# A second tile for turned exponentials, their split one step later, and a fourth tile for first weight parts in the first mixer

## The chip, the cores and the metric

The kernel runs on one core of one Trainium2 chip. The metric is the device time of one execution, in microseconds; the times shown are medians of several executions. A core has five engines with a list of instructions each: TensorE (PE in the profile, its weight loads PEld), VectorE (DVE), ScalarE (ACT), GpSimd (POOL) and SyncE (SP). An engine works through its list in order, and waits on semaphores for what other engines or transfers deliver.

## The reference

Two layers of a decoder trunk for 256 tokens of width 2048, in float32. Each layer adds a mixer and then a gated feed-forward network to the residual stream:

```
for l in range(2):
    h = rms_norm(x, mix_norm[l])
    h = mixer_ab(h, ...) if l == 0 else mixer_c(h, ...)
    x = x + h
    h = rms_norm(x, ffn_norm[l])
    x = x + conv_ffn(h, ...)
```

`mixer_ab` projects to 6144 columns. One half of it is a gated unit that mixes tokens within chunks of 128 (8 heads), the other a gated linear recurrence (8 heads of 128). `mixer_c` is softmax attention with 16 heads of 128, normalised queries and keys, a forgetting gate that adds differences of a cumulative sum `c` to the scores, and an output gate:

```
s = q @ k.T * scale + c[query] - c[key]
p = softmax(where(causal, s, -inf))
o = (p @ v) * sigmoid(g)
```

## The kernel before, in words

**Weights and accuracy.** TensorE multiplies in a rounded float32 format. To keep accuracy, each factor is split into a rounded first part and a remainder, and three of the four products are added. Weights come in chunks of 128 x 1024 numbers (512 KB): SP issues the load into a tile `w` (L191), ScalarE rounds it into `wh` (L178), VectorE subtracts to get the remainder `wl` (L179), and TensorE then runs twelve matmuls of 512 columns on the chunk (L305 to L307 or L324 to L326), four of each kind. The tiles of a chunk are handed out by `three` (L164): four `w`, three `wh` and three `wl` in turn. In mixer C and in the feed-forward layers `deep` names a further pool, and some chunks take tiles from it: in mixer C every fourth chunk takes its `wh` and `wl` there (`more` is 1).

**The clock of the kernel.** Side work is written as Python generators. `tick` (L128) is called once ahead of each chunk and advances each generator in flight by one step, at most `depth[0]` of them at once. So a `yield` is one chunk of weights, and `LAG` (6) of them are left between the issue of a move and the first use of what it brings.

**The order of the lists.** A planner draws up each engine's list at compile time from the order in the program, which acts as priority, and from estimated times. Three helpers add order edges: `in_order` keeps the weight parts in sequence, `held` (L368) puts an instruction behind the last `wh` or `wl` that the program has issued so far, and `tied` puts small matmuls behind the last large one. On the chip the lists are fixed and only semaphores decide.

**First mixer.** `project_first` computes the first projection while the input still arrives. Then follow `mixes` (squares for a norm in a tile `junk`, L557), eight recurrences `hgrn` with products on VectorE and small copies `E` on ScalarE (L695), whose matmuls are L712, L719 and L741 to L743, and `values` (L762), whose projection reads activations in reversed order from a tile `ar` that GpSimd copies. This mixer has no further pool for weight tiles.

**Mixer C.** Four groups of four heads. A group projects queries, keys and values, eight chunks each. Query and key pieces are copied from PSUM to `z` (L1079), squared into `junk` and summed (`sumsq`, L396), scaled, transposed in blocks of 32 by VectorE into `tmp` (L337) and moved into `turn` by sixteen small transfers that SP and GpSimd share (L344). `sums` (L914) makes the cumulative sum `fc` of the forgetting gate once, in small rows; for these it takes two tiles of the tag `pt`. `columns` (L953) turns `fc` with TensorE.

`attend` (L964) handles two heads, in this order of steps: split queries and keys; scores on TensorE, then maximum, exponentials and sums into `sc` (L996 to L1007); two steps on, VectorE transposes blocks of `sc` into `ptmp` (L1014); a step later GpSimd issues sixteen moves from `ptmp` to `pt` (L1023), which make up the turned exponentials; `LAG - 1` steps on, ScalarE and VectorE split them into `ph` and `pl` (L1032, L1033); a step later TensorE multiplies them with the values (L1041, L1044) and ScalarE copies out `o` (L1047). Pairs begin `PAIR` (5) ticks apart. There is one `ptmp`, one `ph`, one `pl` and two `pt`.

Then come four pieces of the output gate (`gate` waits until all heads are done), the output projection and the second feed-forward layer.

Of the kernel before, what the change touches and what calls it, by code (L numbers as in the profile page):

```python
# [8 lines left out]
F32 = mybir.dt.float32  # L9
F32R = mybir.dt.float32r  # L10
# [44 lines left out]
def tile_trunk(ctx: ExitStack, tc: tile.TileContext, x, pp_d, cst_d, mlev_d, msk_d,  # L55
# [107 lines left out]

    def three(n):  # L164
        deep["turn"] += 1
        wpool, pool, nw, ns = wp, wp, 4, 3
        if deep["pool"] is not None:
            if deep["more"] == 2 and deep["turn"] > 12 and deep["turn"] % 5 in (1, 3):
                wpool, pool, nw, ns = deep["pool"], deep["pool"], 2, 2
            elif deep["more"] == 1 and deep["turn"] % 4 == 3:  # L170
                pool, ns = deep["pool"], 1
        w = wpool.tile([P, n], F32, tag="w", name=nm("w"), bufs=nw)
        wh = pool.tile([P, n], F32R, tag="wh", name=nm("wh"), bufs=ns)
        wl = pool.tile([P, n], F32R, tag="wl", name=nm("wl"), bufs=ns)
        return w, wh, wl

# [298 lines left out]
    def mixer_ab(norm):  # L475
# [21 lines left out]
        for g, ps in enumerate(project_first(w_v, norm, lambda: queue.append(finish()))):  # L497
# [5 lines left out]
            else:  # L503
                drain()
                Rt = norm.Rt
                last = ps
        A = norm.a

        def fetch_late(*args):
            r = SC.dma_start(*args)  # L510
# [38 lines left out]
        def mixes():  # L549
            for g in (1, 0):  # L550
                yield
                for T in range(2):
                    held(act(gv[g][:, T], last[T] if g else gv[0][:, T], AF.Gelu, scale=Rt[:, T:T + 1]))
            for g in (1, 0):
                for T in range(2):
                    i = (2 * g + T) * 4
                    j = hp.tile([P, 512], F32, tag="junk", name=nm("junk"), bufs=1)  # L557
                    held(V.tensor_tensor(j, gv[g][:, T], gv[g][:, T], ALU.mult), "wl")
                    V.tensor_reduce(ss[:, i:i + 4], j.rearrange("p (h d) -> p h d", d=P), AX.X, ALU.add)
                    yield  # L560
            yield
            rsq(ss[:, 0:2 * NH], ss[:, 0:2 * NH], P)
            bound()
            for g in range(2):
                yield
                for T in range(2):
                    i = (2 * g + T) * 4
                    v4 = gv[g][:, T].rearrange("p (h d) -> p h d", d=P)
                    held(V.tensor_tensor(v4, v4, ss[:, i:i + 4].unsqueeze(2).to_broadcast([P, 4, P]),
                                         ALU.mult), "wl")  # L570
            yield
            yield
            for h in range(0, NH, 2):
                ps = bank()
                both = [mix(h + i, ps[:, i * S:(i + 1) * S]) for i in range(2)]
                for m in both:
                    next(m)
                for m in both:
                    next(m, None)
                yield  # L580
# [179 lines left out]
        gz = []  # L760

        def values(j):  # L762
            ps = project_tok(w_i[j], norm, lambda: hp.tile([P, 512], F32R, tag="ar", name=nm("ar"), bufs=2))
            itok = hp.tile([P, 2, 512], F32, tag="tok", name=nm("itok"), bufs=2)
            for T in range(2):
                SC.activation(itok[:, T], ps[T], AF.Copy, scale=Rr[:, T:T + 1])
            itoks.append((itok, steps[0]))
# [82 lines left out]
        for q in range(4):  # L850
            if q == 0:

                ps = stretch(0, (0, 2, 4, 6, 8, 10), more=True)
                ahead = stretch(1, (0, 2, 4, 6), more=True)
                stretch(0, (12, 14), ps=ps)
            elif q == 1:
                ps = stretch(1, (8, 10, 12, 14), ps=ahead)
            else:
                ps = stretch(q, range(0, KT, 2))
            z = hp.tile([P, 2, 512], F32, tag="tok", name=nm("zo"), bufs=2)  # L860
            tmp = hp.tile([P, 1024], F32, tag="E", name=nm("tmp"), bufs=2)
            dst = wide("dst").rearrange("p (m t) -> p m t", m=4)
            if q == 0:
                depth[0] = 2
            add_four(q, ps, z, tmp, dst, nxt, 2 if q in (1, 2) else 1, (nc.sync, nc.gpsimd) if q else (nc.gpsimd,))
        es.close()
        banks(ctx, 4)
        return nxt
# [2 lines left out]
    def mixer_c(norm):  # L871
# [39 lines left out]
                PE.matmul(ps[r:r + CH, 0:S], w2[:, k], xT[k], start=k < 4, stop=k >= KT - 4, skip_group_check=True)  # L911
            return ps, pr

        def sums(ps, pr, fc):  # L914
            yield
            yield
            Rq = hp.tile([P, LANE], F32, tag="Rq", name="Rq")
            rows = [hp.tile([P, 6, P], F32, tag="pt", name=nm("rows"), bufs=2)[0:CH].rearrange("p m q -> p (m q)")
                    for _ in range(2)]
            f, fa, on = (rows[0][:, i * S:(i + 1) * S] for i in range(3))  # L920
            R = rows[1][:, 2 * S:3 * S]
            c = rows[1][:, 0:2 * S].rearrange("p (g n) -> p g n", g=2)
            rsq(Rq, pr[:, 0:LANE], D)
            for g in range(4):
                SC.activation(R[:, LANE * g:LANE * (g + 1)], Rq[BLK * g:BLK * g + CH], AF.Copy)
            for g, t in ((1, c[:, 0]), (2, c[:, 1]), (3, f)):
                r = SC.activation(t, ps[BLK * g:BLK * g + CH, 0:S], AF.Copy)
                if g == 1:
                    held(r)
            yield  # L930
            held(V.tensor_tensor(f, ps[0:CH, 0:S], f, ALU.add), "wl")
            for g in range(2):
                V.tensor_tensor(f, f, c[:, g], ALU.add)
            V.memset(fc, 0.0)
            V.memset(on, 1.0)
            V.tensor_tensor(f, f, R, ALU.mult)
            V.tensor_scalar(f, f, pp[0:CH, C_BF:C_BF + 1], None, ALU.add)
            yield
            held(SC.activation(fa, f, AF.Abs))
            act(fa, fa, AF.Exp, scale=-1.0)  # L940
            act(fa, fa, AF.Ln, bias=one1[0:CH])
            V.scalar_tensor_tensor(f, f, 0.0, fa, ALU.min, ALU.subtract)
            V.tensor_tensor_scan(fc[0:CH], on, f, 0.0, ALU.mult, ALU.add)
            cd.append(dp.tile([CH, S], F32, tag="cd", name="cd"))
            nc.gpsimd.dma_start(cd[0], fc[0:CH, :])
            spread(0)

# [16 lines left out]
        def attend(hs, q, k, v, o, rs):  # L964
# [43 lines left out]
                sums.append(sms)  # L1008
            yield
            yield  # L1010
            tmp = hp.tile([P, 6 * P], F32, tag="ptmp", name=nm("ptmp"), bufs=1)
            for i, sms in enumerate(sums):
                V.reciprocal(sms, sms)
                t = V.transpose(tmp.rearrange("p (b m i) -> p b m i", b=4, m=6)[:, :, 3 * i:3 * i + 3],  # L1014
# [6 lines left out]
            for a in range(4):  # L1021
# [3 lines left out]
                                        .rearrange("p (m r) -> p m r", m=6))  # L1025
                if a == 1:
                    yield
            for _ in range(LAG - 1):
                yield
            pair = [hp.tile([P, 2, S], F32R, tag=n, name=nm(n), bufs=1) for n in ("ph", "pl")]  # L1030
            near = pt.rearrange("p (i m) q -> p i (m q)", i=2)[:, :, 0:S]
# [27 lines left out]
        for g in range(CH // 4):  # L1059
            qkv = []  # L1060
            ss = hp.tile([P, 2, 2, LANE // 4], F32, tag="ss", name=nm("ss"), bufs=2)[..., 0:4]
            for j in range(3):
                if g == 0 and j == 2:
                    fc, cd = hp.tile([P, S], F32, tag="fc", name="fc"), []
                    queue.append(sums(*forget(), fc))
                if g and j == 2:
                    spread(g)
                ps = early[j] if g == 0 and j < 2 else project_tok(w_cqkv[j * (CH // 4) + g], norm)
                if j == 2:
                    vs = [hp.tile([P, 512], F32R, tag=n, name=nm(n), bufs=2) for n in ("vh", "vl")]  # L1070
                    v1 = hp.tile([P, 512], F32, tag="v", name=nm("v"), bufs=2)
                    SC.activation(vs[0], ps[0], AF.Copy, scale=Rt[:, 0:1])
                    SC.activation(v1, ps[1], AF.Copy, scale=Rt[:, 1:2])
                    V.scalar_tensor_tensor(vs[1], ps[0], Rt[:, 0:1], vs[0].bitcast(F32), ALU.mult, ALU.subtract)
                    qkv.append((vs, v1))
                    break
                z = piece("z", 2)
                for T in range(2):
                    SC.activation(z[:, T], ps[T], AF.Copy, scale=Rt[:, T:T + 1])  # L1079
                    if j < 2:  # L1080
                        s = hp.tile([P, 512], F32, tag="junk", name=nm("junk"), bufs=1)
                        sumsq(ss[:, j, T], z[:, T], s)
                if j < 2:
                    rsq(ss[:, j], ss[:, j], P)
                    for T in range(2):
                        z4 = z[:, T].rearrange("p (h d) -> p h d", d=P)
                        V.tensor_tensor(z4, z4, ss[:, j, T].unsqueeze(2).to_broadcast([P, 4, P]),
                                        ALU.mult)
                    t = piece("turn", 4)
                    transposed(lambda T: z[:, T], flat(piece("tmp", 2)), heads(t))  # L1090
                    z = heads(t)
                qkv.append(z)
            if g == 0:
                columns(fc)
            os_.append(heads(piece("o", CH // 4)))
            rss.append(hp.tile([P, LANE], F32, tag="rs", name=nm("rs"), bufs=CH // 4)[:, 0:8]
                       .rearrange("p (t h) -> p t h", t=2))
# [282 lines left out]
```

## Time and profile before

| | |
|---|---|
| median of three executions | 2279.82 us (2278.01, 2279.82, 2285.34) |
| the profiled execution, its own time | 2280.85 us |
| its span, first to last instruction | 2279.1 us |
| instructions in the span | 32547 |
| moved by DMA | 483.61 MB, mean 212 GB/s |
| granted TensorE clock | 1.000 |

The span is 1.75 us shorter than the execution's own time; what lies around it is start and end. Profile lines of a group read: source line, engine, operation, tile written <- tiles read, count, then busy us and mean ns of one, then the idle time of the engine just before them with what ended it. A line of a timeline reads: start in us from the beginning of the span, duration in us, engine, line, operation, tiles, and in brackets the idle time before it and its releaser. A releaser is inferred, so a wait for several things can be put down to the wrong one.

### The profile page before, as it was taken

How to read it: one execution, taken by the hardware profiler on the slowest of the kernel's cores; microseconds unless marked ns; L12 is line 12 of the kernel's file. 1: busy time of each engine (PE TensorE's matmuls, PEld its weight loads, DVE VectorE, ACT ScalarE, POOL GpSimd, SP SyncE). 2: the span in 40 equal slices, each digit the busy share in tenths (PEclk: the TensorE clock that was granted, in tenths of full speed). 3: DMA queues.
4: the chain of work that ended last, by engine and by line, in shares of the span. 5: the costliest groups of instructions: out<-in, count | busy, mean ns of one | idle time of the engine just before them, and what ended most of it. 6: DMA issues, size and time to landing. Idle time of an engine off the chain costs nothing.

```text
span 2279.1 us, 32547 instructions
## 1 busy us (share of the span) xinstructions
PE 2271.9 (100%) x10786; PEld 1885.7 (83%) x10786; DVE 1584.5 (70%) x2361; ACT 1300.2 (57%) x1954; POOL 437.9 (19%) x798
## 2 busy tenths in 40 slices
PE   9999999999999999999999999999999999999999
PEld 8888888888888888888888888888888888888887
DVE  7788767767467656766877776776776476667766
ACT  7677655656456445654565555655665465455642
POOL 0120231221012002111133344211211012012102
PEclk9999999999999999999999999999999999999999
DMA  8655767777567666776667667777777676666766
GB/s 288 201 169 164 216 204 229 242 217 228 193 207 224 200 207 197 232 216 189 224 212 227 207 193 213 220 225 222 224 224 213 191 225 203 221 203 199 235 200 180
DMA packets 492617, 483.61 MB, mean 212 GB/s; under 512 B 115136, under 2 KB 460240, under 8 KB 492320
## 3 DMA queue, kind: packets, MB, share of 16 engines
q1 hardware_dynamic: 465888, 453.27, 63.4%
q0 software_dynamic: 24832, 25.92, 5.0%
q10 hardware_dynamic: 1728, 2.35, 0.3%
q8 instruction: 84, 1.38, 0.3%
q14 instruction: 85, 0.70, 0.1%
HBM read 435.24 MB, written 2.11 MB: 192 GB/s over the span
## 4 chain that ended last, share of the span: by engine, by line
PE 97%; DVE 1%; DMA 1%; ACT 1%; issue 0%; POOL 0%; SPq 0%; ACTq 0%; DVEq 0%
PE pm L324 26%; PE pm L325 26%; PE pm L326 26%; PE pm L306 4%; PE pm L305 4%; PE pm L307 4%; PE pm L279 2%; PE pm L205 1%; PE pm L282 1%; PE pm L229 1%; DVE wl L179 0%; DMA turn<-tmp 0%; PE px L991 0%; POOL turn L344 0%; ACT wh L178 0%
## 5 line engine op out<-in xcount | busy, mean ns | idle before, releaser
L179 DVE TENSOR_TENSOR wl<-w,wh 128x1024 fp32r<-128x1024 f32 (+1 forms) x820 | 994.1, 1218 | 546.3 <-ACT wh L178 515.2
L178 ACT ACTIVATE wh<-w 128x1024 fp32r<-128x1024 f32 (+1 forms) x820 | 859.8, 1053 | 698.7 <-PE pm L326 562.5
L324 PE MATMUL pm<-wh,a 128*128 128x512 f32 x1728 | 674.2, 390 | 0.0
L325 PE MATMUL pm<-wl,a 128*128 128x512 f32 x1728 | 673.2, 390 | 0.8 <-DVE wl L179 0.8
L326 PE MATMUL pm<-wh,a 128*128 128x512 f32 x1728 | 673.0, 389 | 0.0
L344 POOL DMA_DIRECT2D zt<-tmp x413 | 223.5, 549 | 1201.7 <-DVE tmp L337 1134.8
L325 PEld LDWEIGHTS pm<-wl,a 128*128 128x128 f32 x1728 | 324.5, 188 | 68.0 <-DVE wl L179 1.3
L326 PEld LDWEIGHTS pm<-wh,a 128*128 128x128 f32 x1728 | 324.5, 188 | 67.4
L324 PEld LDWEIGHTS pm<-wh,a 128*128 128x128 f32 x1728 | 324.5, 188 | 67.3 <-ACT wh L178 0.3
L325 PE MATMUL pm<-wl,hid 128*128 128x512 f32 x688 | 267.9, 389 | 0.0
L324 PE MATMUL pm<-wh,hid 128*128 128x512 f32 x688 | 267.9, 389 | 0.0
L326 PE MATMUL pm<-wh,hid 128*128 128x512 f32 x688 | 267.9, 389 | 0.0
L306 PE MATMUL pm<-wl,a 128*128 128x512 f32 x416 | 162.7, 391 | 1.1 <-DVE wl L179 1.1
L305 PE MATMUL pm<-wh,a 128*128 128x512 f32 x416 | 163.0, 392 | 0.0
L307 PE MATMUL pm<-wh,a 128*128 128x512 f32 x416 | 162.3, 390 | 0.0
L325 PEld LDWEIGHTS pm<-wl,hid 128*128 128x128 f32 x688 | 129.2, 188 | 26.8
L324 PEld LDWEIGHTS pm<-wh,hid 128*128 128x128 f32 x688 | 129.2, 188 | 26.8
L326 PEld LDWEIGHTS pm<-wh,hid 128*128 128x128 f32 x688 | 129.2, 188 | 26.7
L344 POOL DMA_DIRECT2D turn<-tmp x160 | 86.7, 550 | 308.5 <-DVE tmp L337 238.1
L1180 ACT ACTIVATE conv<-zt,pp 128x256 f32<-128x256 f32 x176 | 95.8, 589 | 41.1 <-DMA zt<-tmp 26.0
L1181 DVE SCALAR_TENSOR_TENSOR conv<-zt,pp,conv 128x255 f32<-128x255 f32 x176 | 79.6, 479 | 35.4 <-ACT conv L1180 28.6
L337 DVE STREAM_TRANSPOSE tmp<-z 128x512 f32<-128x512 f32 x120 | 82.9, 703 | 20.4 <-ACT z L1166 16.7
(256 smaller groups left out, 2154.7 us busy)
## 6 DMA issues: line engine op xcount, KB each, us to landing
w<-in_w_up SPq DMA_DIRECT2D x352, 512.0 KB, 4.8
w<-in_w_dn SPq DMA_DIRECT2D x176, 512.0 KB, 4.9
w<-in_w_cqkv SPq DMA_DIRECT2D x96, 512.0 KB, 4.7
w<-in_w_abo SPq DMA_DIRECT2D x32, 512.0 KB, 4.7
w<-in_w_cg SPq DMA_DIRECT2D x32, 512.0 KB, 4.9
w<-in_w_co SPq DMA_DIRECT2D x32, 512.0 KB, 4.7
zt<-tmp SPq DMA_DIRECT2D x414, 32.0 KB, 2.2
zt<-tmp POOLq DMA_DIRECT2D x413, 32.0 KB, 2.0
```

The source lines that it names most:

```text
L178: r = deep["wh"] = SC.activation(wh, w, AF.Copy)
L179: deep["wl"] = V.tensor_tensor(wl, w, wh.bitcast(F32), ALU.subtract)
L305: PE.matmul(ps[T], ah, h, start=k + i == 0, stop=False)
L306: PE.matmul(ps[T], ah, l, start=False, stop=False)
L307: deep["last"] = PE.matmul(ps[T], al, h, start=False, stop=k + i == KT - 1)
L324: PE.matmul(ps[T], ah, h, start=not begun and k + i == ks[0], stop=False)
L325: PE.matmul(ps[T], ah, l, start=False, stop=False)
L326: deep["mm"] = deep["last"] = PE.matmul(ps[T], al, h, start=False, stop=not more and k + i == ks[-1] + 1)
L337: V.transpose(tmp.rearrange("p (b m i t) -> p b m i t", b=4, m=4, t=2)[:, :, :, :, T], src(T).rearrange("p (m b j) -> p b m j", m=4, b=4))
L344: queues[(a + b) % len(queues)].dma_start(dst[BLK * b:BLK * (b + 1), :, a * n:(a + 1) * n], tmp[BLK * a:BLK * (a + 1), b * 4 * n:(b + 1) * ...
L1180: held(SC.activation(c, z, AF.Identity, bias=pp[:, cb:cb + 1], scale=w(2)))
L1181: V.scalar_tensor_tensor(c[:, 1:], z[:, :S - 1], w(1), c[:, 1:], ALU.mult, ALU.add)
```

## The change

- In `attend`, `ptmp` has two tiles in place of one, and `LAG` steps in place of `LAG - 1` lie between the moves and the split into `ph` and `pl`.
- In `mixer_c` the cumulative sum `fc` has no tile of its own any more: it is the first 256 columns of the second `pt` tile that `sums` takes, handed on through the list `cd`. The squares of queries and keys go into the first half of `tmp`, the tile that their transposes write later, so `tmp` is taken before the squares, and `junk` is gone.
- The first mixer opens a further pool after its first projection. Every fourth chunk takes its `wh` there; its `w` and `wl` come from the usual pool.
- In the first mixer `junk` has two tiles in place of one, and the reversed activations use these two; the tag `ar` with its two tiles is gone.

```
 def three(n):
     deep["turn"] += 1
-    wpool, pool, nw, ns = wp, wp, 4, 3
+    wpool, pool, nw, ns, hpool, nh = wp, wp, 4, 3, None, 3
...
+        elif deep["more"] == 0 and deep["turn"] % 4 == 3:
+            hpool, nh = deep["pool"], 1
     w = wpool.tile([P, n], F32, tag="w", name=nm("w"), bufs=nw)
-    wh = pool.tile([P, n], F32R, tag="wh", name=nm("wh"), bufs=ns)
+    wh = (hpool or pool).tile([P, n], F32R, tag="wh", name=nm("wh"), bufs=nh if hpool else ns)
...
+    deep.update(pool=es.enter_context(tc.tile_pool(name="aw", bufs=1)), turn=0, more=0)
...
-                j = hp.tile([P, 512], F32, tag="junk", name=nm("junk"), bufs=1)
+                j = hp.tile([P, 512], F32, tag="junk", name=nm("junk"), bufs=2)
...
-    ps = project_tok(w_i[j], norm, lambda: hp.tile([P, 512], F32R, tag="ar", name=nm("ar"), bufs=2))
+    ps = project_tok(w_i[j], norm, lambda: hp.tile([P, 512], F32R, tag="junk", name=nm("ar"), bufs=2))
...
+    deep["pool"] = None
...
-        rows = [hp.tile([P, 6, P], F32, tag="pt", name=nm("rows"), bufs=2)[0:CH].rearrange("p m q -> p (m q)")
+        full = [hp.tile([P, 6, P], F32, tag="pt", name=nm("rows"), bufs=2).rearrange("p m q -> p (m q)")
                 for _ in range(2)]
+        rows = [t[0:CH] for t in full]
+        fc = full[1][:, 0:S]
+        cd.append(fc)
...
-        cd.append(dp.tile([CH, S], F32, tag="cd", name="cd"))
+        cd.insert(0, dp.tile([CH, S], F32, tag="cd", name="cd"))
...
-        tmp = hp.tile([P, 6 * P], F32, tag="ptmp", name=nm("ptmp"), bufs=1)
+        tmp = hp.tile([P, 6 * P], F32, tag="ptmp", name=nm("ptmp"), bufs=2)
...
-        for _ in range(LAG - 1):
+        for _ in range(LAG):
             yield
...
-            z = piece("z", 2)
+            z, tmp = piece("z", 2), flat(piece("tmp", 2))
...
-                    s = hp.tile([P, 512], F32, tag="junk", name=nm("junk"), bufs=1)
-                    sumsq(ss[:, j, T], z[:, T], s)
+                    sumsq(ss[:, j, T], z[:, T], tmp[:, 0:512])
...
-                transposed(lambda T: z[:, T], flat(piece("tmp", 2)), heads(t))
+                transposed(lambda T: z[:, T], tmp, heads(t))
```

More of the change, by code (lines that the diff above doesn't have):

```diff
@@ L912, in forget, with sums @@
             return ps, pr
-        def sums(ps, pr, fc):
+        def sums(ps, pr):
             yield
@@ L1063, in mixer_c @@
                 if g == 0 and j == 2:
-                    fc, cd = hp.tile([P, S], F32, tag="fc", name="fc"), []
-                    queue.append(sums(*forget(), fc))
+                    cd = []
+                    queue.append(sums(*forget()))
                 if g and j == 2:
@@ L1093, in mixer_c @@
             if g == 0:
-                columns(fc)
+                columns(cd[1])
             os_.append(heads(piece("o", CH // 4)))
```

## Prediction

> **What bounds the kernel now.** The first thing to read on the page is how the engines share the span, then the table of who waited for whom, for TensorE alone (columns: total us, times, longest).
>
> ```profile
> PE 2271.9 (100%) x10786; PEld 1885.7 (83%) x10786; DVE 1584.5 (70%) x2361; ACT 1300.2 (57%) x1954; POOL 437.9 (19%) x798
> ```
> ```profile
> PE pm L306 <- DVE wl L179: 1.1, 2, 0.9
> PE warm L145 <- DVE ones L85: 1.1, 1, 1.1
> PE pm L325 <- DVE wl L179: 0.8, 1, 0.8
> ```
>
> TensorE is busy for 2271.9 of 2279.1 us. All its waits in the list are 3.0 us, and 1.1 of that is the start. The other 1.9 us are three waits for `wl`, the second part of a weight chunk, which VectorE makes from what ScalarE leaves. So before the diff is read, one bound stands: a change that only takes waits away has about 2 us of listed waits to win, out of 2279.
>
> A matmul's end is modelled, so a short stall can hide in a bar that looks busy. The pace from start to start shows it. First the pace without stalls, in the first feed-forward layer: nineteen matmuls, of which the first, two in the middle and the last stand here.
>
> ```profile
> 699.77 0.39 PE L326 MATMUL pm<-wh,a 128*128 128x512 f32 x1
> ...
> 700.23 0.39 PE L325 MATMUL pm<-wl,a 128*128 128x512 f32 x1
> 700.45 0.39 PE L326 MATMUL pm<-wh,a 128*128 128x512 f32 x1
> ...
> 703.85 0.39 PE L326 MATMUL pm<-wh,a 128*128 128x512 f32 x1
> ```
>
> 18 steps in 4.08 us are 0.227 us each (single steps are printed as 0.22 or 0.23), so a chunk of twelve, which is one tick of the kernel's clock, is 2.72 us. The same reading at the three waits, from the timeline of TensorE:
>
> ```profile
> 1192.94 0.39 PE L305 MATMUL pm<-wh,a 128*128 128x512 f32 x1
> 1194.19 0.50 PE L306 MATMUL pm<-wl,a 128*128 128x512 f32 x1 [0.86 <-DVE wl L179]
> 1194.53 0.40 PE L307 MATMUL pm<-wh,a 128*128 128x512 f32 x1
> ```
> ```profile
> 1294.09 0.39 PE L305 MATMUL pm<-wh,a 128*128 128x512 f32 x1
> 1294.72 0.50 PE L306 MATMUL pm<-wl,a 128*128 128x512 f32 x1 [0.24 <-DVE wl L179]
> ```
> ```profile
> 1420.07 0.50 PE L324 MATMUL pm<-wh,a 128*128 128x512 f32 x1
> 1421.33 0.51 PE L325 MATMUL pm<-wl,a 128*128 128x512 f32 x1 [0.76 <-DVE wl L179]
> ```
>
> At 1192.94 the step is 1.25 us instead of 0.227: 1.02 us lost, and the step behind it (0.34) loses 0.11 more. At 1294.09 it is 0.63, so 0.40 lost; at 1420.07 it is 1.26, so 1.03 lost. With 0.11 for the restart of each, the three places cost 1.13 + 0.51 + 1.14 = 2.78 us. That is what can be won there, and all three lie in mixer C (the attention layer).
>
> The busy time by stretches says whether anything else is short (columns: length, then busy us of TensorE, its weight loads, VectorE, ScalarE, GpSimd; granted clock; DMA share; GB/s).
>
> ```profile
> 100.00:250.00 150.00, 150.00 (x1281) 126.25 (x1280) 118.91 (x257) 110.68 (x281) 27.10 (x42) 1.00 0.58 176
> 700.00:720.00 20.00, 20.00 (x90) 16.57 (x89) 13.87 (x23) 11.37 (x16) 4.33 (x8) 1.00 0.80 234
> 1180.00:1200.00 20.00, 19.14 (x94) 15.88 (x93) 13.83 (x26) 9.30 (x19) 11.26 (x21) 1.00 0.65 202
> 1420.00:1440.00 20.00, 19.24 (x89) 15.80 (x89) 14.77 (x18) 12.24 (x17) 4.42 (x9) 1.00 0.80 237
> ```
>
> The clock is 1.00 throughout. An undisturbed stretch has weight loads busy for 16.57 of 20 us; the two stretches with the large waits have 15.88 and 15.80. The first mixer (100 to 250 us) has 126.25 of 150, more than 16.57 in 20, and no wait of TensorE. It has nothing to give back.
>
> **Why TensorE waits in mixer C.** The timeline of ScalarE around the first wait, then around the last, and `wl` on VectorE:
>
> ```profile
> 1181.11 1.06 ACT L178 ACTIVATE wh<-w 128x1024 fp32r<-128x1024 f32 x1 [1.66 <-PE pm L307]
> ...
> 1189.90 0.64 ACT L1032 ACTIVATE ph<-pt 128x512 fp32r<-128x512 f32 x1 [5.02 <-DMA pt<-ptmp]
> 1190.43 1.05 ACT L178 ACTIVATE wh<-w 128x1024 fp32r<-128x1024 f32 x1
> ```
> ```profile
> 1418.43 0.63 ACT L1032 ACTIVATE ph<-pt 128x512 fp32r<-128x512 f32 x1 [8.29 <-DMA turn<-tmp]
> 1418.96 3.89 ACT L178 ACTIVATE wh<-w 128x1024 fp32r<-128x1024 f32 x4
> ```
> ```profile
> 1192.95 1.18 DVE L179 TENSOR_TENSOR wl<-w,wh 128x1024 fp32r<-128x1024 f32 x1
> ```
>
> ScalarE takes its list in order. `ph`, the first part of the turned exponentials, stands at its head and waits 5.02 and 8.29 us for their move to land (the second is put down to another transfer, but `ph` reads only `pt`). The next `wh` stands behind it; `wl` needs that `wh`, and TensorE needs `wl`. The waits of 1141 to 1425 us in total:
>
> ```profile
> ACT ph L1032 <- DMA turn<-tmp: 23.4, 4, 8.3
> ACT ph L1032 <- DMA pt<-ptmp: 13.7, 4, 5.0
> ```
> ```profile
> DVE ptmp L1014 <- DMA pt<-ptmp: 9.0, 4, 3.7
> ```
>
> Each of the eight pairs of heads stops ScalarE, 37.1 us together, and in four of them VectorE also stops, 9.0 us, because the transposes of the next pair want the one `ptmp` tile that the moves still read.
>
> **The change, part by part.** *Split one tick later (LAG).* No instruction is added. For each of eight pairs, one `ph`, one `pl`, the eight matmuls behind them and two copies of the result move by a tick. `ph` is tied behind the last `wh` that the program has issued, so it should now stand behind one more `wh`: at 1189.90 behind the one that ran at 1190.43. That `wh` (1.05 us) then runs in ScalarE's idle time ahead of the landing, its `wl` follows, and the chunk wanted at 1193 is ready some microseconds early. The chunk after it is wanted 2.72 us later, and has only 0.64 of `ph`, 1.05 of `wh` and 1.2 of `wl` after the landing. So a landing as late as now costs nothing at these two places: −1.13 and −1.14 us. The wait at 1294 has another cause:
>
> ```profile
> 1292.26 1.30 DVE L337 STREAM_TRANSPOSE tmp<-z 128x512 f32<-128x512 f32 x2
> 1293.48 1.18 DVE L179 TENSOR_TENSOR wl<-w,wh 128x1024 fp32r<-128x1024 f32 x1
> ```
>
> There `wl` stands behind the transposes of a key piece, which the change leaves where they are. Its 0.51 us stays. The later matmuls of the pair read `pl` with a long lead:
>
> ```profile
> 1190.56 0.69 DVE L1033 TENSOR_TENSOR pl<-pt,ph 128x512 fp32r<-128x512 f32 x1
> ```
> ```profile
> 1197.45 0.48 PE L1044 MATMUL px<-pl,vh 128*128 128x256 f32 x2
> ```
>
> From the end of `pl` at 1191.25 to its use at 1197.45 are 6.2 us; even if only `pl` moved by 2.72, 3.5 would remain. The last pair ends a tick later and the gates wait for it, but by the code the first gated tile is made about tick 25 after the last value piece and read at tick 33; one tick more changes nothing.
>
> *Second `ptmp`.* It takes away the 9.0 us of VectorE's wait, all inside the chain to the next landing. Behind it in VectorE's list stand `pl` and `wl`; they gain, and next late is the move itself. GpSimd issues the moves one by one:
>
> ```profile
> L1023 POOL DMA_DIRECT2D pt<-ptmp x128 | 71.6, 568 | 109.3 <-ACT wh L178 50.7 <-ACT z L1079 19.0 <-DVE ptmp L1014 17.9
> ```
>
> Sixteen times 0.568 are 9.1 us a pair, unchanged, and two pairs in a group's 65 us leave room. TensorE sees none of it beyond what is counted above: 0, by bounds of −0.5 (the wait at 1294 goes too) and 0.
>
> *`fc` in a `pt` tile, squares in `tmp`.* The same instructions write other places. `fc` holds the second `pt` tile until its transposes on TensorE, before the first pair asks for one. `tmp` is taken before the squares, not after; its two tiles alternate, and the one wanted was emptied a group ago, so the square waits for nothing. `junk` and `fc` give back what the second `ptmp` takes. 0 us.
>
> *First mixer.* Every fourth `wh` has its own tile, so ScalarE may run four chunks ahead where three was the end. No instruction is added; `w` and `wl` keep their tiles, so loads on SP's queue are not issued earlier. There is no wait to remove: 0. Sharing `junk` and `ar` is 0, as the squares are over before reversed activations are wanted. The price to fear is a `wh` of 1.04 us put ahead of the small copies `E`, each of which a product chain on VectorE waits for:
>
> ```profile
> 118.89 1.04 ACT L178 ACTIVATE wh<-w 128x1024 fp32r<-128x1024 f32 x1
> ```
> ```profile
> 122.78 0.29 DVE L705 TENSOR_TENSOR kq<-kq,tot 128x128 f32<-128x128 f32 x1
> ```
> ```profile
> 130.92 0.38 PE L712 MATMUL px<-kq 128*128 128x128 f32 x2
> ```
>
> The first head's chain ends at 123.07 and TensorE reads it at 130.92: 7.85 us of cover. One `wh` ahead of each of the seven pairs of copies would be 7.3 us, still hidden.
>
> The sum: −1.13 − 1.14 + 0 + 0 + 0 = −2.3 us, so 2278.6 for the profiled execution, whose own time was 2280.85. The median of the three runs is 1.03 us lower, 2279.82; carried to it, the forecast is **2277.5 us**.
>
> **Where the Trainium skill says otherwise.** By the Trainium skill ("Trainium Kernel Development and Optimization", Best Practices), busy matmuls say little about headroom and the busy share of weight loads says more; here that is 83%. And "TensorE: Matmul & The Clock Gate" ("Wait — 56ns, not 53.3ns?") gives 215.7 ns from start to start for 512 columns at full clock, against our 227; 11 ns on some 9,700 such matmuls would be an estimated 110 us. The measurement speaks against a part of that being in reach: at 700 us nothing waits and the pace is 0.227 all the same.
>
> **Rivals.**
> 1. *The wait only moves, or the split stays where it is* in ScalarE's list. For it: the landing, not the list, ends the wait, and the planner may fill the tick otherwise. Against: `ph` stood right ahead of one `wh`. Time: 2279.8, less at most 0.5.
> 2. *The split lands in a crowd (slower).* In four of eight pairs the split moves past the end of a key piece, where ScalarE and VectorE copy, square, scale and transpose it, and at 1294 `wl` has no lead at all. Where `wl` leads its matmul by less than 0.63 + 0.69 = 1.32 us (the rows at 1418.43 and 1190.56), `ph` and `pl` ahead of it lengthen TensorE's wait by up to that. All eight: 10.6, less the 2.3 won: 2288.1. Four: 5.3, so 2282.8. Against it: the 37.1 us of waiting shrink by as much as 2.72 a pair.
> 3. *The first mixer's chains come late (slower).* Two `wh` ahead of each pair of copies are 14.6 us, 6.7 beyond the cover, eight heads: +54, so 2331. Against it: ScalarE has 39 us idle in those 150.
> 4. *The pace itself falls* in mixer C because weights lie ready earlier: if every step of its 160 chunks (1,920 matmuls) were the 0.22 that some steps show, 7 ns each, that is −13, with the 2.3 2264. No stretch of the trace has such a mean pace. This is the direction in which the Trainium skill's 215.7 ns points.
>
> **How the numbers follow.** A measurement of this kernel tells about 0.3% from no change, 6.8 us: faster is below 2273.0, slower above 2286.7. Chances: forecast 0.51, rival 1 0.18, rival 2 0.22 (0.15 of it with seven pairs or more, above 2286.7), rival 3 0.05, rival 4 0.04. So faster 0.04, within 0.3% 0.76, slower 0.20. The three runs of before lie −1.8 and +5.5 us about their median; the range goes from 2273.5 (forecast less 4) to 2288.5 (rival 2 with all eight), leaving out rivals 3 and 4 and the edge of rival 2.
>
> **What would show it.** Right: no wait of TensorE near 1193 and 1420, weight loads at 16.5 or more in both stretches, `ph` behind one more `wh` and its total wait well under 37.1 us, no wait of the `ptmp` transposes, and the wait near 1294 still there. Wrong: waits for `wl` of a microsecond at the starts of value pieces (rival 2), waits at L712, L719 or L741 in the first mixer (rival 3), or a pace other than 0.227.

## The result, and the profile after

The changed kernel takes 2284.94 us (median of 22 executions, 2281.15 to 2288.24), the kernel before 2279.84 (22 executions beside them). The ratio is 1.0019, with a 95% interval of 1.0013 to 1.0026: the change costs **5.1 us**, 2279.84 to 2284.94, where −2.3 us were forecast. The profiled execution of the changed kernel took 2282.67 us, one of its shorter ones, with a span of 2280.6. Between it and before's profiled execution (2280.85) lie 1.8 of the 5.1 us; the traces show the kind of the loss, the medians its size.

Lines have moved by 2 to 7: `wh` is L180 (L178 before), `wl` L181, the matmuls L307 to L309 and L326 to L328, `ph` L1039 (L1032), `pl` L1040, the moves L1030, the copies of `z` L1086. First the page and the waits of TensorE (total us, times, longest).

```profile
PE 2271.5 (100%) x10786; PEld 1884.8 (83%) x10786; DVE 1581.2 (69%) x2361; ACT 1299.5 (57%) x1954; POOL 436.8 (19%) x798
```
```profile
PE pm L308 <- DVE wl L181: 2.2, 2, 1.5
PE warm L145 <- DVE ones L85: 1.1, 1, 1.1
PE pm L327 <- DVE wl L181: 0.8, 1, 0.8
```

The busy shares tell nothing: they are those of before. The three waits for `wl` are still three, and larger: 3.0 us where they were 1.9. Where they lie is in the timeline of TensorE:

```profile
1319.12 0.39 PE L307 MATMUL pm<-wh,a 128*128 128x512 f32 x1
1320.17 0.50 PE L308 MATMUL pm<-wl,a 128*128 128x512 f32 x1 [0.66 <-DVE wl L181]
...
1337.61 0.39 PE L307 MATMUL pm<-wh,a 128*128 128x512 f32 x1
1339.54 0.50 PE L308 MATMUL pm<-wl,a 128*128 128x512 f32 x1 [1.54 <-DVE wl L181]
...
1424.33 0.51 PE L326 MATMUL pm<-wh,a 128*128 128x512 f32 x1
1425.59 0.50 PE L327 MATMUL pm<-wl,a 128*128 128x512 f32 x1 [0.75 <-DVE wl L181]
```

Read as in the prediction (step less 0.227, and 0.11 for the restart), they cost 0.93 + 1.82 + 1.14 = 3.89 us; the three of before cost 2.78. None is left near 1193 or at 1294. The stretches say the same (length, busy us of TensorE, weight loads, VectorE, ScalarE, GpSimd; clock; DMA share; GB/s):

```profile
1180.00:1200.00 20.00, 20.00 (x98) 16.86 (x97) 16.60 (x33) 10.96 (x21) 13.06 (x24) 1.00 0.74 234
1320.00:1340.00 20.00, 18.29 (x84) 15.04 (x85) 14.18 (x27) 9.67 (x17) 10.58 (x20) 1.00 0.58 182
1420.00:1440.00 20.00, 19.25 (x89) 15.70 (x88) 12.63 (x13) 11.42 (x15) 6.50 (x12) 1.00 0.78 207
```

The first stretch is now undisturbed, with weight loads at 16.86; 1320 to 1340 is the new bad one, and 1420 to 1440 is as bad as before.

### What stands behind the split now

The waits of ScalarE for the landing, 1141 to 1425 us, have barely shrunk, 34.4 us in place of 37.1:

```profile
ACT ph L1039 <- DMA turn<-tmp: 22.7, 4, 8.1
...
ACT ph L1039 <- DMA pt<-ptmp: 11.7, 4, 5.2
```

The place with the largest loss, in ScalarE's list, before and after (a line with "sc" is an exponential, of the second head here):

```profile
1331.02 0.63 ACT L1032 ACTIVATE ph<-pt 128x512 fp32r<-128x512 f32 x1 [3.96 <-DMA pt<-ptmp]
1331.55 1.04 ACT L178 ACTIVATE wh<-w 128x1024 fp32r<-128x1024 f32 x1
1332.50 0.39 ACT L99 ACTIVATE sc<-sc,mxs 128x128 f32<-128x128 f32 x1
...
1333.38 1.24 ACT L1079 ACTIVATE z<-pm,Rt 128x512 f32<-128x512 f32 x2
```
```profile
1326.97 1.06 ACT L180 ACTIVATE wh<-w 128x1024 fp32r<-128x1024 f32 x1 [0.15 <-ACT sc L99]
1333.28 0.63 ACT L1039 ACTIVATE ph<-pt 128x512 fp32r<-128x512 f32 x1 [5.25 <-DMA pt<-ptmp]
1333.82 0.39 ACT L99 ACTIVATE sc<-sc,mxs 128x128 f32<-128x128 f32 x1
...
1334.70 1.24 ACT L1086 ACTIVATE z<-pm,Rt 128x512 f32<-128x512 f32 x2
1335.84 2.94 ACT L180 ACTIVATE wh<-w 128x1024 fp32r<-128x1024 f32 x3
```

`ph` did move behind one more `wh`, here and at all eight pairs. But the `wh` it moved behind was the only thing that stood between it and the second head's exponentials. Before, the weights came first after a landing: `wh` 0.53 us behind `ph`. Now two exponentials and the two copies of a query piece come first, and the next `wh` starts 2.56 us behind `ph`. VectorE adds to it:

```profile
1334.83 0.17 DVE L1020 RECIPROCAL rs<-rs 128x2 f32<-128x2 f32 x1 [5.12 <-ACT sc L99]
...
1336.01 0.57 DVE L1021 STREAM_TRANSPOSE ptmp<-sc 128x384 f32<-128x384 f32 x1
...
1337.07 0.68 DVE L1040 TENSOR_TENSOR pl<-pt,ph 128x512 fp32r<-128x512 f32 x1
...
1338.27 1.22 DVE L181 TENSOR_TENSOR wl<-w,wh 128x1024 fp32r<-128x1024 f32 x1
```

Transposes, squares and `pl` that hang on those exponentials and copies are ahead of `wl`. From `ph` to the end of `wl` are 1338.27 + 1.22 − 1333.28 = 6.2 us. TensorE wanted that `wl` at 1337.84, 4.6 us after `ph` had started.

Before, the same stretch took 4.2 us at the first pair of every group, and TensorE wanted the `wl` 4.3 us after `ph` here. So with a landing as late as before, one tick more would have left about 7 us, and 6.2 would have fitted. By these numbers the stop of 1337 needs both: the longer stretch behind the landing, and a landing that is itself 2.26 us later (1333.28 in place of 1331.02). The moves of this pair start 2.45 us later than before (1318.88 in place of 1316.43). The same delay makes the stop at 1319, which has no split near it (the nearest run at 1275.15 and 1333.28):

```profile
1308.18 1.06 ACT L180 ACTIVATE wh<-w 128x1024 fp32r<-128x1024 f32 x1 [2.48 <-DMA w<-in_w_cqkv]
```
```profile
1318.90 4.61 DVE L181 TENSOR_TENSOR wl<-w,wh 128x1024 fp32r<-128x1024 f32 x4
```

ScalarE waits 2.48 us for a load of weights, shortly behind key pieces that came 2.84 us later than before (1303.20 in place of 1300.36). From there on VectorE's scores (1312.51 in place of 1310.06), the first head's exponentials, the moves and this `wl` are all 2.45 us later. What made the load late isn't shown.

The second price is a chain. The second head's exponentials that now wait for one landing are those of the next pair, whose transposes, moves and landing follow from them. For the last two pairs, ScalarE's list after:

```profile
1404.14 0.63 ACT L1039 ACTIVATE ph<-pt 128x512 fp32r<-128x512 f32 x1 [4.18 <-DMA pt<-ptmp]
1404.68 0.39 ACT L99 ACTIVATE sc<-sc,mxs 128x128 f32<-128x128 f32 x1
...
1422.69 0.63 ACT L1039 ACTIVATE ph<-pt 128x512 fp32r<-128x512 f32 x1 [8.12 <-DMA turn<-tmp]
1423.23 2.94 ACT L180 ACTIVATE wh<-w 128x1024 fp32r<-128x1024 f32 x3
```

and GpSimd's issue of the last pair's moves, before and after:

```profile
1403.51 2.23 POOL L1023 DMA_DIRECT2D pt<-ptmp  x4 [5.92 <-ACT z L1133]
```
```profile
1407.00 2.23 POOL L1030 DMA_DIRECT2D pt<-ptmp  x4 [6.51 <-PE pm L328]
```

The moves start 3.49 us later, as those exponentials do (1404.68 in place of 1401.20). The last of the sixteen starts 2.03 us later (1417.07), and `ph` runs at 1422.69 in place of 1418.43, 4.26 later; so 2.2 us of this came only behind the last issue. One tick is 2.72, and TensorE itself is 0.52 (below) + 0.93 + 1.82 − 1.13 − 0.51 = 1.63 us later there: 4.35 together. In this execution the landing moved along with the split, so the wait at 1420 is the same wait, one chunk on. That isn't so in every one: in the four other profiles below with this place of the split, the `wl` behind this landing is wanted 1.9 to 3.1 us after `ph` (1.9 here; 2.8 are needed), and where it is 3.1, in the later split alone, TensorE doesn't stop.

### The profile page after: what moved, and what is told of

It is laid out like the page before. It is cut to its first block, busy times and chain, and to the rows that moved or that the text cites. A ratio compares the mean times of both kernels' runs of the same rounds, so it can differ in the third digit from the quotient of the medians.

```text
span 2280.6 us, 32616 instructions
## 1 busy us (share of the span) xinstructions
PE 2271.5 (100%) x10786; PEld 1884.8 (83%) x10786; DVE 1581.2 (69%) x2361; ACT 1299.5 (57%) x1954; POOL 436.8 (19%) x798
## 4 chain that ended last, share of the span: by engine, by line
PE 94%; DMA 2%; DVE 2%; ACT 1%; issue 1%; POOL 1%; SPq 0%; DVEq 0%; ACTq 0%
PE pm L326 26%; PE pm L327 26%; PE pm L328 26%; PE pm L308 4%; PE pm L307 4%; PE pm L309 4%; PE pm L207 1%; PE pm L281 1%; DMA pt<-ptmp 1%; PE pm L284 1%; DVE wl L181 1%; PE pm L231 0%; ACT wh L180 0%; POOL pt L1030 0%; DMA turn<-tmp 0%
## 5 line engine op out<-in xcount | busy, mean ns | idle before, releaser
L181 DVE TENSOR_TENSOR wl<-w,wh 128x1024 fp32r<-128x1024 f32 (+1 forms) x820 | 992.7, 1216 | 539.5 <-ACT wh L180 475.0
L180 ACT ACTIVATE wh<-w 128x1024 fp32r<-128x1024 f32 (+1 forms) x820 | 859.9, 1053 | 694.7 <-PE pm L328 545.2
L326 PE MATMUL pm<-wh,a 128*128 128x512 f32 x1728 | 673.7, 390 | 0.0
L328 PE MATMUL pm<-wh,a 128*128 128x512 f32 x1728 | 672.4, 389 | 0.0
L326 PEld LDWEIGHTS pm<-wh,a 128*128 128x128 f32 x1728 | 324.3, 188 | 67.5 <-ACT wh L180 0.3
L328 PEld LDWEIGHTS pm<-wh,a 128*128 128x128 f32 x1728 | 324.3, 188 | 67.5
L326 PE MATMUL pm<-wh,hid 128*128 128x512 f32 x688 | 267.6, 389 | 0.0
L328 PE MATMUL pm<-wh,hid 128*128 128x512 f32 x688 | 267.6, 389 | 0.0
L307 PE MATMUL pm<-wh,a 128*128 128x512 f32 x416 | 162.9, 392 | 0.0
L309 PE MATMUL pm<-wh,a 128*128 128x512 f32 x416 | 162.1, 390 | 0.0
L328 PEld LDWEIGHTS pm<-wh,hid 128*128 128x128 f32 x688 | 129.1, 188 | 26.9
L326 PEld LDWEIGHTS pm<-wh,hid 128*128 128x128 f32 x688 | 129.1, 188 | 26.8
```

Of the source, the lines that this page charges most:

```text
L180: r = deep["wh"] = SC.activation(wh, w, AF.Copy)
L181: deep["wl"] = V.tensor_tensor(wl, w, wh.bitcast(F32), ALU.subtract)
L307: PE.matmul(ps[T], ah, h, start=k + i == 0, stop=False)
L309: deep["last"] = PE.matmul(ps[T], al, h, start=False, stop=k + i == KT - 1)
L326: PE.matmul(ps[T], ah, h, start=not begun and k + i == ks[0], stop=False)
L328: deep["mm"] = deep["last"] = PE.matmul(ps[T], al, h, start=False, stop=not more and k + i == ks[-1] + 1)
```

## The experiments

The theories that the expectations name, in words: the loss comes from the first mixer's fourth `wh` tile; or from the later split, because of what its wait holds up in the list; or from the edits around it in mixer C (the second `ptmp`, the shared tiles). Kernels that ran side by side shared the executions of the kernel before, so each ratio is against those. Edits are shown against the changed kernel or against before, as said, and only the lines that matter.

### The first mixer alone

The changed kernel with mixer C as before: one `ptmp`, `LAG - 1`, `fc` and the squares in tiles of their own.

```
-            tmp = hp.tile([P, 6 * P], F32, tag="ptmp", name=nm("ptmp"), bufs=2)
+            tmp = hp.tile([P, 6 * P], F32, tag="ptmp", name=nm("ptmp"), bufs=1)
...
-            for _ in range(LAG):
+            for _ in range(LAG - 1):
...
-                        sumsq(ss[:, j, T], z[:, T], tmp[:, 0:512])
+                        sumsq(ss[:, j, T], z[:, T], hp.tile([P, 512], F32, tag="junk", name=nm("junk"), bufs=1))
```

> The first mixer's part alone: every fourth chunk's first part in its own tile, reversed activations in the squares' tiles; mixer C as before. Theory A (the fourth tile lets the planner deal the first mixer's lists anew, and TensorE then waits for chains that were in time before, as at 192.9 us and at the diagonal matmuls near 203 us in the profile after): most of the 5.1 us, so +3 to +6 us, with waits of TensorE between 100 and 250 us. Theory B (the loss is mixer C's): within 1.2 us of before, the 0.76 us that the profile shows in this stretch.

Measured: 2279.97 against 2279.99 us, ratio 1.0000 (0.9991 to 1.0009). The first mixer isn't the cause of the loss; a part of up to 2 us can't be excluded by this interval.

### Mixer C alone

The changed kernel without the `aw` pool, with `junk` and `ar` as before.

```
-        deep.update(pool=es.enter_context(tc.tile_pool(name="aw", bufs=1)), turn=0, more=0)
```

> Mixer C's part alone: second tile for turned exponentials, split a step later, sums and squares in other tiles; first mixer as before. Theory A: no loss here, -2 to +0.7 us. Theory B (the split a step later only hands the wait for the landing to the next chunk, and the four waits of 0.8 to 1.7 us at 1319, 1337 and 1424 us of the profile after vary from execution to execution): +3 to +6 us, with waits for the second weight part between 1180 and 1430 us.

Measured: 2283.28 us, ratio 1.0013 (1.0004 to 1.0021). Most of the loss is here, 3.3 us.

### All but the later split

```
-            for _ in range(LAG):
+            for _ in range(LAG - 1):
```

> All of the change but the later split (LAG - 1 steps again). Theory B with the later split at fault: close to before, -1 to +1 us. Theory B with the second tile at fault (earlier transposes, moves issued in another rhythm): +4 to +6 us as the whole change. Theory A: +3 to +6 us, as the first mixer's part is still in it.

Measured: 2280.33 us, ratio 1.0001 (0.9992 to 1.0010). Without the later split there is no loss to be seen. The trace has the old waits back, at 1193, 1294 and 1421 us, and a smaller one at 1350.

### All but the second `ptmp`

```
-            tmp = hp.tile([P, 6 * P], F32, tag="ptmp", name=nm("ptmp"), bufs=2)
+            tmp = hp.tile([P, 6 * P], F32, tag="ptmp", name=nm("ptmp"), bufs=1)
```

> All of the change but the second tile for turned exponentials; the split stays a step later. Theory B with the later split at fault: +4 to +6 us. Theory B with the second tile at fault: -1 to +1 us. Theory A: +3 to +6 us.

Measured: 2284.69 us, ratio 1.0016 (1.0007 to 1.0025). The loss doesn't come from the second tile, and the second tile doesn't lessen it.

### The later split alone, and other steps

Three kernels that are before with one number changed, and the changed kernel once more:

```
-            for _ in range(LAG - 1):
+            for _ in range(LAG):
```

> The kernel before with one edit, the split a step later (LAG steps for LAG - 1). If the later split is the whole loss: +3.5 to +5.5 us, as the whole change. If it costs only together with the other tiles for sums and squares: -2 to +1 us. The forecast's own theory, that it removes the waits at 1193 and 1420 us: -2.3 us.

Measured: 2284.01 against 2279.81 us, ratio 1.0013 (1.0005 to 1.0022). That one line costs 4.2 of the 5.1 us. Its profiled execution, 2284.07 us, is a typical one; five stops in mixer C and a slight sixth at 1371, read as above, sum to 4.7 us. None is at 1424. The waits of TensorE, 1141 to 1430 us:

```profile
PE pm L308 <- DVE wl L181: 2.9, 4, 1.4
```

```
+            for _ in range(LAG + 1):
```

> The kernel before with the split two steps later. If each step hands the wait for the landing on to work with less lead (the loss grows with the step): +7 to +11 us. If two steps are enough for the moves to land (the waits of ScalarE before the split, 37 us in all now, fall under 15 us): -3 to 0 us.

Measured: 2278.35 us, ratio 0.9993 (0.9984 to 1.0002). One step more and the loss is gone: TensorE has no wait in mixer C. `ph` now stands behind the exponentials, the two copies and one more `wh`, and its waits fall to 4.6 us, 0.8 of them without a releaser and the rest these:

```profile
ACT ph L1039 <- DMA turn<-tmp: 2.0, 1, 2.0
ACT ph L1039 <- DMA pt<-ptmp: 1.8, 1, 1.8
```

```
+            for _ in range(LAG - 2):
```

> The kernel before with the split one step earlier (LAG - 2). If the position of the split has a best place and the kernel before is at it: +2 to +8 us, with longer waits of ScalarE before the split. If earlier is better for the chain that hangs on it (second head's exponentials, their transposes, the next pair's moves): -2 to 0 us.

Measured: 2278.63 us, ratio 0.9996 (0.9987 to 1.0004), no wait in mixer C; the second expectation came out. In the trace `ph` stands at the same place of the list as before; only copies of `o` come earlier. Its waits are 25.6 us (37.1 before), and the first landing comes 2.9 us earlier than before, although the lists up to it are the same. Why this kernel is calm stays open.

> The whole change once more, for a second profile. Its times spread from 2281.2 to 2288.2 us; if the spread comes from mixer C, the waits of TensorE between 1180 and 1430 us differ from the first profile's 3.9 us by as much as the two times differ; if it comes from elsewhere, they agree and the difference lies outside.

Measured: 2283.95 us for the one execution, with stops of TensorE of 1.04 us at 1320 and 1.91 at 1339 again (without the 0.11 for the restart). The changed kernel had them at 1319 and 1338, the later split alone at 1321 and 1340: the same two places in three profiled executions, so not one execution's accident. Mixer C alone and the kernel with one `ptmp` have the second stop too, at 1338 and 1337, and not the first; in their traces ScalarE waits at most 0.43 us for the load for which it waits 2.48 to 2.94 us in the other three. As to the expectation, the stops in mixer C sum to 4.6 us here against 3.9 in the first profile: 0.7 of the 1.28 us between the two executions come from there, the rest from elsewhere.

### The edge alone: `ph` behind the exponentials

The changed kernel with nothing but one more order edge. `ph` is tied behind the last exponential that the program has issued, as well as behind the last `wh`.

```
-                    act(scf[:, a:b], scf[:, a:b], AF.Exp, bias=mxs[:, T:T + 1], accum_out=sms[:, T])
+                    deep["ex"] = act(scf[:, a:b], scf[:, a:b], AF.Exp, bias=mxs[:, T:T + 1], accum_out=sms[:, T])
...
-            held(SC.activation(pair[0], near, AF.Copy))
+            r = SC.activation(pair[0], near, AF.Copy)
+            held(r)
+            held(r, "ex")
```

> The whole change, with one order edge more: the split stands behind the last exponential that the program has issued, so that on ScalarE's list the second head's exponentials of the next pair come ahead of it (and the first copy of the query piece too); the chunk behind it stays behind it. Theory C (the wait for the landing, up to 8 us, also holds back the exponentials behind it, so the next pair's moves and what follows start late): at least 3 us of the 5.1 come back, 2278 to 2282 us; the time from the first to the second head's exponentials of every second pair falls from 4 to 8 us to about 2. Theory D (only the next first weight part behind the split matters): no change, 2283.5 to 2286 us.

Measured: 2279.03 against 2279.93 us, ratio 0.9995 (0.9986 to 1.0003). All waits of TensorE in mixer C are gone; these are left:

```profile
PE warm L145 <- DVE ones L85: 1.1, 1, 1.1
PE pm L284 <- DVE wl L181: 0.4, 1, 0.4
PE px L682 <- ACT st L727: 0.3, 1, 0.3
```

The same place in ScalarE's list:

```profile
1327.59 0.39 ACT L99 ACTIVATE sc<-sc,mxs 128x128 f32<-128x128 f32 x1
...
1328.47 0.67 ACT L1088 ACTIVATE z<-pm,Rt 128x512 f32<-128x512 f32 x1
1332.27 0.63 ACT L1039 ACTIVATE ph<-pt 128x512 fp32r<-128x512 f32 x1 [3.13 <-DMA pt<-ptmp]
1332.81 0.67 ACT L1088 ACTIVATE z<-pm,Rt 128x512 f32<-128x512 f32 x1
1333.38 2.95 ACT L180 ACTIVATE wh<-w 128x1024 fp32r<-128x1024 f32 x3
```

The exponentials run at 1327.59, in ScalarE's idle time ahead of the landing, where the changed kernel had them at 1333.82, behind it. `wh` is 1.11 us behind `ph` instead of 2.56, and the next pair's moves start at 1331.18 instead of 1337.25. From the first head's exponentials to the second's are 2.1 us, 8.0 in the changed kernel. From `ph` to the end of the next `wl` are 3.4 us in place of 6.2, and TensorE wants it after 5.2. At the last pair, 2.8 us are needed and 6.8 there. Same instructions, same number of steps, one edge: 5.9 us less than the changed kernel's median.

This is the run that shows the cause, the exponentials behind the wait. All four kernels that have them right behind `ph` (the change, mixer C alone, one `ptmp`, the later split alone) take 3.3 to 5.1 us more than before; of the eight others, none is slower by more than 0.9. It doesn't say how much each of the two prices is worth, as the edge takes both away.

### The copies as well

The same, and `ph` of the first pair of each group also behind both copies of the query or gate piece.

```
+            if hs[0] % 4 == 0:
+                held(r, "z")
...
-                    SC.activation(z[:, T], ps[T], AF.Copy, scale=Rt[:, T:T + 1])
+                    deep["z"] = SC.activation(z[:, T], ps[T], AF.Copy, scale=Rt[:, T:T + 1])
```

> As the one before, and the split of each first pair also stands behind both copies of the query piece. Theory C: as that one or up to 1.5 us better, 2277.5 to 2281 us. Theory D: 2283.5 to 2286 us.

Measured: 2278.43 us, 2277.97 to 2278.98, ratio 0.9993 (0.9984 to 1.0002). The waits of `ph` are down to 9.4 us. Beside it before's executions go from 2277.57 to 2286.31: all eleven executions of this version lie within 1.0 us of each other. That it is shorter than before isn't shown, as its interval includes 1.

### The change with two steps

```
-            for _ in range(LAG):
+            for _ in range(LAG + 1):
```

> The whole change with the split two steps later in place of one: behind exponentials, copies and one more first weight part. Theory C and theory D both: 2277.5 to 2279.5 us, as the kernel before with the same split (2278.35). It is the version that should beat both kernels, by up to 1.5 us over the one before; the second tile then takes away the last wait of the transposes, 4.8 us on VectorE, worth nothing to TensorE.

Measured: 2278.87 us, ratio 0.9996 (0.9987 to 1.0005). The whole change without its loss, 6.1 us below the changed kernel's median; no transpose into `ptmp` waits. That it beats the kernel before, as expected, isn't shown, as the interval includes 1.

### Before with the edge

Before, with the edge of the exponentials, one `ptmp` and `LAG - 1`.

> The kernel before (split at its old step, one tile) with the order edge alone: the exponentials ahead of the split. Theory C: the waits at 1193, 1294 and 1420 us go, 2277.5 to 2279 us, 1 to 2 us faster than before. Theory D: the first weight part that stood behind the split stands ahead of it as well, so this run cannot tell by its time alone; ScalarE's wait before the split would then stay at 25 us or more.

Measured: 2280.83 us, 2279.46 to 2285.68, ratio 1.0004 (0.9995 to 1.0013), though the waits at 1193, 1294 and 1420 did go. This is a miss: 2277.5 to 2279 was expected from the list's order. (ScalarE's wait before the split is 15.7 us, not the 25 or more of theory D.) One new stop takes their place:

```profile
1222.94 0.39 PE L307 MATMUL pm<-wh,a 128*128 128x512 f32 x1
1225.47 0.50 PE L308 MATMUL pm<-wl,a 128*128 128x512 f32 x1 [2.14 <-DVE wl L181]
...
1227.56 0.63 PE L309 MATMUL pm<-wh,a 128*128 128x512 f32 x1
1227.98 0.63 PE L307 MATMUL pm<-wh,a 128*128 128x512 f32 x1
```

ScalarE's list ahead of it:

```profile
1213.88 0.52 ACT L986 ACTIVATE qq<-turn 128x128 fp32r<-128x128 f32 x2 [4.51 <-DMA turn<-tmp]
1214.32 1.04 ACT L180 ACTIVATE wh<-w 128x1024 fp32r<-128x1024 f32 x1
...
1220.71 0.21 ACT L99 ACTIVATE ss<-rm 128x8 f32<-128x8 f32 x1 [2.70 <-DVE rm L391]
...
1221.07 2.94 ACT L180 ACTIVATE wh<-w 128x1024 fp32r<-128x1024 f32 x3
```

It is the same thing at two other waiting instructions: `qq` stands 4.51 us for its transfer and `ss` 2.70 us for VectorE, each with a `wh` right behind it. The kernel with the edge and the second `ptmp` has another `wh` ahead of `ss` there and doesn't stop. Curing one wait of the list thus moved weights behind two others. Whether this stop comes in every execution isn't known; the median of 2280.83, against 2278.4 to 2279.0 for the kernels without a stop in mixer C, suggests that something like it is usual.

## Why the prediction was wrong

- **What bounds the kernel** held: 100% TensorE, few and short waits, all in mixer C, and only microseconds to win. The result lies within the range given, 2273.5 to 2288.5, and within 0.3% of before.
- **The step that failed is "Split one tick later", −1.13 − 1.14.** `ph` did move behind one more `wh` at all eight pairs. The sentence that fell is that the chunk after it "has only 0.64 of `ph`, 1.05 of `wh` and 1.2 of `wl` after the landing", 2.9 us. The trace shows 6.2 (1333.28 to 1339.49), because the exponentials, copies, transposes and squares that had stood behind that `wh` now stand ahead of the next one. Where the landing leaves more than 6.2 us the wait is gone (1193: 8.3 us from `ph` at 1188.46 to the use at 1196.75), so the term −1.13 came true there. Where it leaves 4.6 there is a larger one (1337); the landing is 2.26 us later there, and 6.2 us would have fitted ahead of TensorE without that. The 2.9 us were too few even for the list of before, and the prediction's own rows say so: `ph` starts at 1189.90 and `wl` ends at 1192.95 + 1.18, 4.2 us later. What fills them is in VectorE's list of before, the transposes of the second head's exponentials ahead of `wl`:

```profile
1192.38 0.17 DVE L1013 RECIPROCAL rs<-rs 128x2 f32<-128x2 f32 x1 [1.13 <-ACT sc L99]
1192.47 0.56 DVE L1014 STREAM_TRANSPOSE ptmp<-sc 128x384 f32<-128x384 f32 x1
```

- **"A landing as late as now costs nothing"** failed at the second place too: the landing doesn't stay where it was. The next pair's exponentials stand behind the wait, the last landing went 4.26 us later, and the 1.14 us came back whole in this execution. The rows for the chain were in the trace of before: the exponentials at 1332.50 stood close behind the `wh` that `ph` was to pass.
- **The wait at 1294 "stays"**: wrong in the trace of the changed kernel, where it is gone. The change doesn't leave the transposes where they are in VectorE's list: one `wl` more, at 1290.64, now runs ahead of them (1293.60). In the later split alone smaller stops stand near it, 0.29 and 0.45 us at 1291 and 1297.
- **Second `ptmp`, 0**: right. The 9.0 us of VectorE's wait went. With the later split `rs` waits 11.2 us for the exponentials in four of the pairs instead (4.3 before); in the kernel that has the second tile without the later split it is 4.5, so the second tile isn't what makes `rs` wait.
- **`fc` and the squares, 0**: right as far as can be told, 2280.33 for the kernel that has them without the later split.
- **First mixer, 0**: right at the median (1.0000). In the profiled execution one wait of 0.4 us at 193 us (a stop of 0.52) and one of 0.3 at L682 are new; both are inside what the median can't tell.
- **Rival 2** came nearest, 2282.8 to 2288.1 for four to eight crowded pairs. Its mechanism, other work between `ph` and the weights, is the one found. Its price wasn't: not 1.32 us at each of many pairs, but 0.93, 1.82 and 1.14 at three places, and the crowd is what `ph` holds back, not what it comes between. That 2284.94 lies in its range is luck. The chances, 0.22 for this rival against 0.51, were the wrong way round.

What stays open: which part of the later landings is the chain and which the transfer itself (from the end of the last issue of a pair's moves to its `ph` are 1.7 to 5.1 us in the changed kernel, 2.0 to 3.5 before), what made the load of weights at 1308 late (with it, the third group's first pair is hit; the first two groups' leave 8.3 and 9.1 us), why one step earlier is calm, and 0.9 us between the later split alone (+4.2) and the whole change (+5.1), which the intervals don't separate.

## What to carry to other kernels

An instruction that waits for a transfer at the head of an in-order list is priced by everything that stands behind it, so before it is moved past one neighbour, write down who comes next in the list and who waits for those. Moving it by one step can be worse than by none or by two; better is an edge that names what must stay ahead of it, and then the same question for the next waiting instruction of the same list. If what is held back produces the next wait's own input, the wait travels with the move, and a gain of "one tick" is not to be counted.

## What the runs showed of the hardware

A stop of TensorE can cost more than its length. Behind the stop of 2.31 us in the kernel before with the edge, seven steps take 0.427 us in place of 0.227, among them the one from 1227.56 to 1227.98, and one at either end is part way: 1.6 us more. The first mixer alone, whose profiled execution happens to be its longest, 2285.94 us, shows the same behind two stops of 1.14 and 1.03 us in a row. The granted clock (third figure from the end) in a stretch of each:

```profile
1227.20:1229.90 2.70, 2.70 (x8) 2.13 (x7) 1.62 (x2) 0.00 (x0) 1.73 (x4) 0.50 0.56 115
```
```profile
1426.00:1428.00 2.00, 2.00 (x6) 1.56 (x5) 2.00 (x2) 1.70 (x3) 0.00 (x0) 0.50 0.88 271
```

The stop of 1.71 us in the changed kernel has no such tail, the steps behind it are 0.33 and 0.24 us; nor has that of 1.91 us in its second profile. The Trainium skill ("TensorE: Matmul & The Clock Gate", Part 1 and "Wait — 56ns, not 53.3ns?") has the clock halve after an idle window of about 3.4 us, and 426.7 ns from start to start for 512 columns at half clock. The step agrees with the 0.427 us here; the length doesn't quite, as a stop of 2.31 us was enough.

That one step of the split stands apart from its neighbours (2278.63 one step earlier, 2279.81 before, 2284.01 one later, 2278.35 two later) was not expected either; the other three don't differ clear of the noise.
